# RWKV-7 units of a hybrid flow-matching step cut into jobs that are joined by events, with a matmul order made beside a model of the other engines' queues

## The chip, the core and the metric

The kernel runs on one NeuronCore of a Trainium2 chip. The metric is the device time of one execution in microseconds (us). Engines are named as in the profile: PE (TensorE), DVE (VectorE), ACT (ScalarE), POOL (GpSimd), SP (the queue that issues the DMAs). Each takes its own instructions in order.

## The reference, cut to what matters

One layer is computed for 128 context tokens and 512 latent tokens, 640 columns in all, with width 2048. The combined input projection feeds attention (8 heads) and a bidirectional RWKV-7 mixer (16 heads of 64); both are joined by an output projection, a norm and a SwiGLU feed-forward part.

```python
def _latent_layer(x, c, ckv_ctx, krope_ctx, s_fwd, s_bwd, p):
    sh1, sc1, g1, sh2, sc2, g2 = _adaln(c, p["w_mod"], p["b_mod"])
    proj = (x * (1 + sc1) + sh1) @ p["w_in"]
    ...
    att = _attend_blocked(q_nope, q_rope, ...)
    rw, _, _ = _rwkv_mixer(proj[..., OFF_RW:], s_fwd, s_bwd, p)
    x = _post_norm(x, g1, _merge(att, rw, p), p["ln1_g"], p["ln1_b"])
    x = _post_norm(x, g2, _swiglu(x * (1 + sc2) + sh2, p), p["ln2_g"], p["ln2_b"])
    return x

def step(S, inp):                      # the RWKV scan, one token
    r_t, w_t, k_t, v_t, kk_t, a_t = inp
    sa = jnp.einsum("bhvk,bhk->bhv", S, -kk_t)
    S = S * w_t[:, :, None, :] + sa[..., None] * (kk_t * a_t)[:, :, None, :] + v_t[..., None] * k_t[:, :, None, :]
    return S, jnp.einsum("bhvk,bhk->bhv", S, r_t)
```

The scan is done for both directions; `r_t`, `w_t` and the rest are functions of the projection (token shift, decay and rate through small low-rank products, a normalised key).

## The kernel before, in words

Stages. (1) 0 to about 250 us: the adaLN products `x<-wm,cs`, fed from HBM in pieces, and the first input projection tiles. (2) To about 1145 us: `main()` makes the rest of the input projection, tile by tile (96 matmuls of 128x320 into one `acc` pair of PSUM banks, in three passes of split operands, names `xh`, `xl`, `whi`, `wlo`). Later adaLN products and the RWKV mixer stand between these matmuls. (3) To about 1480 us: attention, and what is left of RWKV. (4) To the end: output projection, norms and the feed-forward part (tiles `b`), with the same code in both kernels.

RWKV. The 16 heads are 8 pairs of 128 rows; each pair is scanned in two halves `j` of 320 columns, so there are 16 units. A unit is scanned in chunks of 64 tokens, five per direction. Its steps: `rwkv_load` (per pair: low-rank weights `lw`, key norm `kk`), `rwkv_decays` (matmuls `m<-xw,lw` and `m<-xa,lw`, then tanh, scan, exp), `rwkv_prep` (DVE and POOL make `nk` and `pr`), `rwkv_grams` (matmuls `m<-pr,nk`, evacuated to `mab`, `mrb`, `pr`), `inverse` (a long row of DVE instructions on `it` and `ip`, ending in `tc`, then matmuls `m<-tc,mab`, `m<-pm,uc`, `m<-t,mab`, `m<-u,pm`), `rwkv_turned` (transposes `sv`, `zv`, `bk`), `rwkv_chain` (five steps in series, each matmuls `m<-sv,pr`, `m<-xs,uf`, `m<-zv,bk` with an evacuation behind each), and per pair `rwkv_bonus` and `rwkv_post` (group norm and gate, `m<-sg,gw`, tile `y`).

What sets the order. PE runs in the order in which the Python program emits its matmuls. That order is made by `Jobs`: every piece of work is a generator with a rank; the one of lowest rank that is ready runs until it yields, and a yielded number is the time after which it may go on. `Tensor` adds a time for each matmul to `now`. In the kernel before, the yielded numbers are constants in `HOPS` (`"prep": 1.68`, `"inv": 12.0`, ...): one number for all that DVE, ACT and POOL do in that step, whatever else stands in their queues. The order of the other engines' instructions is set by a scheduler behind this program, and it too goes by the program's order. A unit starts its prep when the unit ahead has ended its chain: beside a unit run only the decays of the next one, the bonus and the post. Attention has rank 3 and `main` rank 4, so RWKV goes first wherever it is taken to be ready. PSUM: two `acc` pairs, three single banks `m`, one bank `x`.

## Time and profile before

| | |
|---|---|
| time, 3 runs | 3460.67, 3463.75, 3466.30 us; median 3463.75 |
| span of the profiled execution, first to last instruction | 3458.1 us |
| busy share: PE, PE weight load, DVE, ACT, POOL | 94%, 86%, 72%, 42%, 29% |
| mean granted PE clock | 0.969 |
| PE idle 0 to 250 us, 250 to 1375, 1375 to 1480, 1480 to the end | 28.6, 118.4, 10.6, 46.4 us |
| 16 units: first and last prep (tile `nk`) | 254.8 and 1265.0 us |

No other time than its span is given for the profiled execution; it lies 5.65 us under the median of the runs. In the profile a row of a group reads: line, engine, operation, output<-inputs, shape, count | busy us, mean ns of one | idle us of the engine just before them, and what ended it. A float32 matmul of the program stands as two records in the trace. A row of the timeline reads: start us, length us, engine, line, operation, names, shape, count, and in brackets the idle time before it. The rows themselves stand with the prediction.

### The profile page before, as it was taken

The numbers are of one execution on the slowest core, as the hardware profiler recorded it, in microseconds if no ns is written. First come the engines' busy times: TensorE is split into PE (matmuls) and PEld (weight loads), VectorE is DVE, ScalarE is ACT, GpSimd is POOL, SyncE is SP. The second block draws the span as 40 slices with busy tenths as digits, with TensorE's granted clock in tenths as the row PEclk, the third lists the DMA queues.
The fourth block names the chain that finished last, engine by engine and source line by source line (L and its number), as shares of the span: only waits on it lengthen the run. The fifth ranks groups of instructions, "written<-read, shape, count | busy, mean of one in ns | idle before, by whom it ended". The sixth has DMA issues, their size and how long they took to land.

```text
span 3458.1 us, 70966 instructions
## 1 busy us (share of the span) xinstructions
PE 3254.0 (94%) x27682; PEld 2972.3 (86%) x27682; DVE 2499.6 (72%) x4478; ACT 1449.3 (42%) x3031; POOL 999.1 (29%) x1034
## 2 busy tenths in 40 slices
PE   7988988999999789999979999999999999999998
PEld 4677766777887678989979999999999999999997
DVE  1356766776776666467688988888887778899677
ACT  1144443443444444445453444444444444333234
POOL 0022222222222122102174544444443332222124
PEclk9999999999999799999989999999999999999998
DMA  8754444444221211076534443444343357888643
GB/s 300 246 177 136 147 145 139 158 157 144 78 62 56 73 31 40 29 252 185 154 110 138 165 130 122 145 134 129 125 142 116 118 186 282 298 285 288 222 140 120
DMA packets 284528, 527.71 MB, mean 153 GB/s; under 512 B 30432, under 2 KB 66720, under 8 KB 284192
## 3 DMA queue, kind: packets, MB, share of 16 engines
q1 hardware_dynamic: 284192, 523.18, 46.1%
q8 instruction: 217, 3.56, 0.4%
q14 instruction: 119, 0.97, 0.1%
HBM read 428.99 MB, written 92.44 MB: 151 GB/s over the span
## 4 chain that ended last, share of the span: by engine, by line
PE 58%; DVE 6%; ACT 2%; issue 2%; DMA 1%; POOL 1%; SPq 0%; ACTq 0%; DVEq 0%; POOLq 0%
PE b L114 50%; PE acc L114 4%; PE m L114 2%; DVE z L228 1%; DVE ql L228 1%; POOL z L228 1%; PE x L114 1%; ACT z L240 0%; PE acc L118 0%; DVE smx L1165 0%; DVE pr L228 0%; ACT P L1166 0%; DVE ip L228 0%; DVE raw L228 0%; DMA raw<-in_w_down_dram 0%
## 5 line engine op out<-in xcount | busy, mean ns | idle before, releaser
L228 DVE TENSOR_TENSOR ql<-raw,qh 128x512 fp32r<-128x512 f32 (+1 forms) x1064 | 887.8, 849 | 260.4 <-ACT qh L1303 247.1
L1303 ACT CAST qh<-raw 128x512 fp32r<-128x512 f32 (+1 forms) x1064 | 633.3, 610 | 830.6 <-PE b L114 647.2
L114 PE MATMUL b<-t,qh 128*128 128x320 f32 x2816 | 622.8, 310 | 8.5 <-ACT qh L1303 7.4
L228 POOL TENSOR_TENSOR raw<-raw,raw 128x512 f32<-128x512 f32 x240 | 354.4, 1477 | 804.4 <-DVE ql L228 546.2
L114 PE MATMUL b<-op,qh 128*128 128x320 f32 x2560 | 553.2, 311 | 1.9 <-ACT qh L1303 1.1
L114 PEld LDWEIGHTS b<-t,qh 128*128 128x128 f32 x2816 | 472.6, 189 | 9.7 <-ACT qh L1303 8.1
L114 PE MATMUL b<-p,qh 128*128 128x320 f32 x2112 | 468.9, 311 | 0.0
L114 PE MATMUL b<-t,ql 128*128 128x320 f32 x1408 | 436.1, 310 | 5.6 <-DVE ql L228 5.5
L114 PEld LDWEIGHTS b<-op,qh 128*128 128x128 f32 x2560 | 425.9, 189 | 4.4 <-ACT qh L1303 2.7
L114 PE MATMUL b<-op,ql 128*128 128x320 f32 x1280 | 379.0, 311 | 5.4 <-DVE ql L228 5.3
L114 PEld LDWEIGHTS b<-p,qh 128*128 128x128 f32 x2112 | 356.0, 189 | 0.3
L114 PE MATMUL b<-p,ql 128*128 128x320 f32 x1056 | 329.0, 312 | 6.9 <-DVE ql L228 6.9
L114 PEld LDWEIGHTS b<-t,ql 128*128 128x128 f32 x1408 | 265.0, 188 | 7.8 <-DVE ql L228 7.7
L114 PEld LDWEIGHTS b<-op,ql 128*128 128x128 f32 x1280 | 236.7, 189 | 8.3 <-DVE ql L228 7.9
L114 PE MATMUL b<-mh,qh 128*128 128x320 f32 x1024 | 230.4, 314 | 6.6 <-ACT qh L1303 6.6
L114 PE MATMUL acc<-xh,whi 128*128 128x320 f32 x928 | 230.3, 330 | 3.5 <-ACT P L1166 2.5
L114 PE MATMUL acc<-xl,whi 128*128 128x320 f32 x928 | 232.9, 333 | 0.0
L114 PE MATMUL acc<-xh,wlo 128*128 128x320 f32 x928 | 231.8, 332 | 0.0
L114 PEld LDWEIGHTS b<-p,ql 128*128 128x128 f32 x1056 | 199.8, 189 | 9.6 <-DVE ql L228 9.6
L228 DVE TENSOR_TENSOR raw<-raw,raw 128x512 f32<-128x512 f32 x240 | 185.4, 780 | 12.5 <-POOL raw L228 9.4
L265 ACT CAST whi<-raw 128x512 fp32r<-128x512 f32 (+1 forms) x156 | 94.9, 609 | 226.4 <-PE acc L114 138.9
L114 PEld LDWEIGHTS b<-mh,qh 128*128 128x128 f32 x1024 | 174.5, 191 | 8.3 <-ACT qh L1303 7.8
(330 smaller groups left out, 5654.5 us busy)
## 6 DMA issues: line engine op xcount, KB each, us to landing
wm<-in_w_mod_dram SPq DMA_DIRECT2D x64, 1024.0 KB, 5.3
raw<-in_w_gate_dram SPq DMA_DIRECT2D x188, 256.0 KB, 2.7
raw<-in_w_up_dram SPq DMA_DIRECT2D x188, 256.0 KB, 2.9
op<-hd SPq DMA_DIRECT2D x136, 320.0 KB, 5.4
raw<-in_w_in_dram SPq DMA_DIRECT2D x132, 256.0 KB, 2.7
wm<-in_w_mod_dram SPq DMA_DIRECT2D x64, 512.0 KB, 6.0
raw<-in_w_out_dram SPq DMA_DIRECT2D x128, 256.0 KB, 3.0
raw<-in_w_down_dram SPq DMA_DIRECT2D x128, 256.0 KB, 5.4
```

The lines of the kernel that those rows point to most:

```text
L114: self.eng.matmul(out, lhsT, rhs, start=start, stop=stop)
L228: eng.tensor_tensor(out=out, in0=x, in1=y, op=op)
L265: A.copy(hi, r)
L1303: A.copy(hi, x)
```

## The change

Jobs. `rwkv()` is replaced by `rwkv_chains` (rank 0), `rwkv_inverses` (0.3), `rwkv_turn` (0.5), `rwkv_fed` (prep and grams, 0.6), `rwkv_inputs` and `rwkv_rest` (1). Each goes through the 16 units by itself and waits for events of the others, so the chain of one unit, the inverse of the next and prep or decays of the one after may stand between each other. The grams go to an `acc` pair while `main` runs, not to two of the three `m` banks. The states are loaded in `rwkv_turned`, not in the chain; `r` and `v` of a pair are loaded later than `k`. More buffers: `N_S` 14 for 12, `N_W` 8 for 6; the DMA scratch is smaller.

Times in the planner. `V`, `A` and `G` are wrapped in `Lane`, which keeps the time at which that engine's queue will be empty, from an overhead and a rate per element; a job yields `left(...)`, the time until the queues it has fed are empty. `inverse` and `rwkv_decays` yield after each DVE step. `Tensor` has other times per matmul and adds 0.093 us where the shape of the array's tile changes.

Every engine has the same instructions as before by count and kind, apart from the banks of 13 of 16 units' grams.

```diff
-N_S = 12
+N_S = 14
-N_W = 6
+N_W = 8
+RANK_F = 0.3
+RANK_G = 0.6
...
+class Lane:
+    def __init__(self, eng, pe, fixed, rate):
+        self.eng, self.pe, self.fixed, self.rate, self.free = eng, pe, fixed, rate, 0.0
+    def __getattr__(self, name):
+        f = getattr(self.eng, name)
+        def call(*args, **kw):
+            n = 0
+            for x in (kw.get("out", args[0] if args else None), kw.get("in_")):
+                if x is not None:
+                    n = max(n, math.prod(x.shape[1:]))
+            self.free = max(self.free, self.pe.since) + self.fixed + self.rate * n
+            return f(*args, **kw)
+        return call
...
-    V, A, G, DMA = nc.vector, nc.scalar, nc.gpsimd, nc.sync
+    V, A, G = Lane(nc.vector, T, 0.1, 1.2e-3), Lane(nc.scalar, T, 0.1, 1.05e-3), Lane(nc.gpsimd, T, 0.15, 2.5e-3)
+    def left(*lanes, more=0.15):
+        return max(x.free for x in lanes) - T.now + more
...
     def inverse(...):
-        yield HOP["inv"]
+        yield left(V)
...
-        yield HOP["prep"]
+        yield left(V, A, G)
...
-        yield HOP["pow"]
+        yield left(V, G, more=1.5)
...
     def rwkv_grams(u):
-            both = [mps(), mps()]
+            if mg.done:
+                both = [mps(), mps()]
+            else:
+                pair = acc()
+                both = [pair[:, h, :] for h in range(2)]
...
-    def rwkv():
...
+    def rwkv_fed():
+        for u in UNITS:
+            yield decayed[u]
+            if before(u):
+                yield turns[before(u)]
+            yield from rwkv_prep(*u, shs[u[0]], us[u])
+            prepped[u].done = True
+            yield from rwkv_grams(us[u])
+            grammed[u].done = True
+            jobs.spawn(rwkv_turn(u), TURN)
+    def rwkv_turn(u):
+        if before(u):
+            yield chained[before(u)]
+        yield from rwkv_turned(*u, shs[u[0]], us[u])
+        turns[u].done = True
+    def rwkv_inverses():
+        for u in UNITS:
+            yield grammed[u]
+            us[u]["u"] = yield from inverse(us[u]["mab"], chained[before(u)] if before(u) else None)
+            inverted[u].done = True
+    def rwkv_chains():
+        for u in UNITS:
+            yield turns[u]
+            yield inverted[u]
+            yield from rwkv_chain(*u, shs[u[0]], us[u])
+            chained[u].done = True
```

What moves, at three places. First, PE ahead of the first unit's grams (`pr`, `nk`); before:

```order
L114 MATMUL acc_155<-xl_1365,whi_1992 128x320 x2
L114 MATMUL acc_155<-xh_1364,wlo_1993 128x320 x2
L114 MATMUL acc_155<-xh_1373,whi_1992 128x320 x2
L114 MATMUL acc_155<-xl_1374,whi_1992 128x320 x2
L114 MATMUL m_2111<-pr_2077,nk_2076 128x128
L114 MATMUL m_2112<-pr_2078,nk_2076 128x128
```

and now:

```order
L118 MATMUL acc_2110<-xl_1026,whi_2155 128x320 x2
L118 MATMUL x_2174<-wm_403_2175,cs 32x512 x4
L118 MATMUL acc_2110<-xh_1366,whi_2206 128x320 x2
L118 MATMUL acc_2260<-pr_2180,nk_2179 128x128
L118 MATMUL acc_2260<-pr_2181,nk_2179 128x128
```

Between the last decay matmul (`xl`, `lw`) and these grams stood 11 such `acc` rows and one `x<-wm` row; now there are 49 `acc` rows, three `x<-wm` rows and one `x<-cst,ev` row, and the grams write `acc`, not `m`.

Second, PE in the chain of the first unit (`xs`, `zv`, `sv` are its tiles, `uf` its inverse; `tc`, `pm`, `t` are those of the next unit's inverse, `vr` its transposes); before, from one step's second product to its third and on:

```order
L114 MATMUL m_2856<-xs_2839,uf_166 64x64 x4
L114 MATMUL acc_2566<-xh_1025,whi_2654 128x320 x2
L114 MATMUL acc_2566<-xl_1026,whi_2654 128x320 x2
L114 MATMUL acc_2566<-xh_1025,wlo_2655 128x320 x2
L114 MATMUL m_2869<-zv_2290,bk_2291 64x64 x4
L114 MATMUL acc_2566<-xh_1346,whi_2762 128x320 x2
```

and now:

```order
L118 MATMUL m_3377<-xs_3344,uf_166 64x64 x4
L118 MATMUL m_3385<-tc_3361,mab_2790 32x32 x40
L118 MATMUL m_3427<-zv_2382,bk_2383 64x64 x4
L118 MATMUL m_3436<-pr_2180,sv_2381 64x64
L118 MATMUL m_3436<-pr_2181,sv_2381 64x64
L118 MATMUL m_3437<-pr_2180,sv_2381 64x64
L118 MATMUL m_3437<-pr_2181,sv_2381 64x64
L118 MATMUL m_3436<-mrb_2259,zv_2382 64x64 x2
L118 MATMUL m_3437<-mrb_2259,zv_2382 64x64 x2
L118 MATMUL m_3449<-pm_3384,uc_3325 32x32 x40
L118 MATMUL m_3502<-cst,v_2153 64x64 x10
L118 MATMUL x_3117<-wm_588_3333,cs 32x512 x4
```

A chain step, whose places in between were taken by projection matmuls, now shares them with the next unit's inverse.

Third, DVE in a chain (`zv`, `sv`, `fs`, `y` of the chain; `ip`, `it`, `ue` of an inverse; `ld` of decays); before, in the second unit:

```order
L237 SCALAR_TENSOR_TENSOR sv_3137<-m_3578,dc_2382,sd_3558 64x64 x4
L228 TENSOR_TENSOR wlo_3592<-raw_3506,whi_3591 128x512
L228 TENSOR_TENSOR y_2669<-m_3609,y_2669 128x64
L228 TENSOR_TENSOR y_2669<-m_3610,y_2669 128x64
L896 COPY zv_3138<-m_3621 64x2x64
L237 SCALAR_TENSOR_TENSOR sv_3137<-m_3634,dc_2382,sd_3606 64x64 x4
```

and now, in the fifth:

```order
L148 SCALAR_TENSOR_TENSOR fs_6357<-m_6523,dc_4959,sd_6466 64x64
L148 TENSOR_REDUCE it_6411<-ip_6575 128x2x7
L148 TENSOR_TENSOR ip_6593<-im_6481,it_6411 128x512
L148 TENSOR_REDUCE it_6411<-ip_6593 128x8x8
L148 TENSOR_TENSOR ip_6651<-it_6411 128x512
L148 TENSOR_SCALAR ld_6535<-ld_6535 128x640
L148 TENSOR_REDUCE it_6411<-ip_6651 128x8x8
L148 COPY zv_5763<-m_6586 64x2x64
```

Between one step's state update and the next step's `zv` there was at most a `wlo` and two small `y`; now rows of the sixth unit's inverse and the decays of a third stand there.

More of the change, by code (lines that the diff above doesn't have):

```diff
@@ L100, in __init__, with matmul @@
     def __init__(self, eng):
-        self.eng, self.now = eng, 0.0
-    def matmul(self, out, lhsT, rhs, start, stop, share=1.0):
+        self.eng, self.now, self.last, self.since = eng, 0.0, None, 0.0
+    def matmul(self, out, lhsT, rhs, start, stop):
         n = 1
@@ L145, in step @@
         job = min((j for j in free if j.ready <= now), key=lambda j: j.rank)
-        self.pe.now = now
+        self.pe.now, self.pe.since = now, job.ready
         try:
@@ L556, in step_kernel, with inverse @@
         G.memset(t, 0.0)
-    def inverse(mab):
+    def inverse(mab, before):
         par = [con("par")[:, i: i + 1] for i in range(2)]
@@ L571, in inverse @@
         G.memset(tb[:, 0:256:17], 1.0)
+        yield left(V, A)
         x = half5("ix")
         V.transpose(x, nd)
+        yield left(V, more=0.0)
         x3 = x.rearrange("p (t s) -> p t s", s=32)
@@ L578, in inverse @@
         stt(m3, x3[:, :, 0:16], par[0], m3, ALU.mult, ALU.add)
+        yield left(V, more=0.0)
         t3 = tb[:, :256].rearrange("p (t s) -> p t s", s=16)
@@ L586, in inverse @@
             V.tensor_reduce(out=t8[:, :, t, 0:t], in_=pd, op=ALU.add, axis=AX.X)
+            yield left(V, more=0.0)
         lo8, hi8 = slice(0, 8), slice(8, 16)
@@ L621, in inverse @@
         u, t = h10(u2[:, :HN]), h10(t2[:, :HN])
-        yield HOP["d32b"]
+        yield left(V)
+        if before:
+            yield before
         f4 = ch(full)
@@ L639, in inverse @@
         for lo, hi in lohi:
+            A.copy(f4[lo, :, 0:32], u[lo])
+        for lo, hi in lohi:
             A.copy(f4[lo, :, 32:64], h10(ps2[lo, :HN]))
-        yield HOP["d64b"]
+        yield left(A)
         return full
@@ L706, in rwkv_load, with rwkv_load2 @@
         sh["ks"] = slot("ks")
-        yield HOP["kk"]
+        yield left(V)
         return sh
+    def rwkv_load2(i, sh):
+        for j, n in ((0, "r"), (2, "v")):
+            sh[n] = slot(n)
+            DMA.dma_start(out=sh[n], in_=rkv_d[i][j])
     HV = [slice(0, HN), slice(HN, NT)]
@@ L777, in rwkv_turned @@
         sv_, zv, bk = u["sv"], u["zv"], u["bk"] = wide("sv"), wide("zv"), wide("bk")
-        yield HOP["vr"]
+        for h in range(2):
+            if j == 0:
+                for d, e in ((0, 0), (1, 7)):
+                    DMA.dma_start(out=sv_[rows(h), e, h, :], in_=a["states"][d, i, rows(h)])
+                G.memset(sv_[rows(h), 5, h, :], 0.0)
+            else:
+                G.tensor_copy(sv_[rows(h), 0:6:5, h, :], cy[rows(h)].rearrange("p (d v) -> p d v", v=C))
+                G.memset(sv_[rows(h), 3, h, :], 0.0)
+        yield left(A)
         for d in range(2):
@@ L839, in rwkv_chain @@
             sh["y"] = slot("y")
-        for h in range(2):
-            if j == 0:
-                for d, e in ((0, 0), (1, 7)):
-                    DMA.dma_start(out=sv_[rows(h), e, h, :], in_=a["states"][d, i, rows(h)])
-                G.memset(sv_[rows(h), 5, h, :], 0.0)
-            else:
-                G.tensor_copy(lanes(sv_, h, 0), lane2(cy, h))
-                G.memset(sv_[rows(h), 3, h, :], 0.0)
         y = sh["y"]
@@ L908, in rwkv_chain @@
             if e < 4:
-                yield HOP["p"]
+                yield left(V)
         outputs(4)
@@ L950, in rwkv_post @@
             tt(V, y[:, hs], y[:, hs], ps[:, :HN], ALU.mult)
-            yield HOP["gup"]
+            yield left(V)
         DMA.dma_start(out=mix_d[8 + i], in_=y)
-    def rwkv():
-        def start(i):
+    UNITS = [(i, j) for i in range(npairs) for j in range(2)]
+    shs = [None] * npairs
+    us = {}
+    decayed, prepped, turns, grammed, inverted, chained = ({u: jobs.event() for u in UNITS} for _ in range(6))
+    posted, summed_ = ([jobs.event() for _ in range(npairs)] for _ in range(2))
@@ L972, in rwkv @@
-        sh, u = yield from start(0)
-        last = None
-        for i in range(npairs):
-            for j in range(2):
-                yield from rwkv_prep(i, j, sh, u)
-                yield from rwkv_grams(u)
-                turned = jobs.spawn(rwkv_turned(i, j, sh, u), TURN)
-                side = jobs.spawn(beside_second(i, sh) if j else beside_first(i, sh, last), RANK_S)
-                u["u"] = yield from inverse(u["mab"])
-                yield turned
-                yield from rwkv_chain(i, j, sh, u)
-                last = (i, sh)
-                yield side
-                if side.result:
-                    sh, u = side.result
```

143 lines of the change are left out of this document (94 added, 49 removed).

## The prediction

> **What bounds the kernel now.** I read the head of the page first, then a table by stages, then the groups of PE with the idle time before them, and last single waits.
>
> ```profile
> PE 3254.0 (94%) x27682; PEld 2972.3 (86%) x27682; DVE 2499.6 (72%) x4478; ACT 1449.3 (42%) x3031; POOL 999.1 (29%) x1034
> ...
> PEclk9999999999999799999989999999999999999998
> ...
> PE 58%; DVE 6%; ACT 2%; issue 2%; DMA 1%; POOL 1%; SPq 0%; ACTq 0%; DVEq 0%; POOLq 0%
> ```
>
> PE is busy for 94% of the span of 3458.1 us and makes most of the chain that ended last, so time can come from two places only: PE's idle 204 us, and what a low granted clock adds to its busy time. By stages (columns: stretch, its length, busy us of each engine, granted clock, DMA share, GB/s):
>
> ```profile
> 0.00:250.00 250.00, 221.40 (x1266) 149.16 (x1267) 87.44 (x172) 61.31 (x117) 14.50 (x45) 0.96 0.72 243
> 250.00:1035.00 785.00, 713.86 (x9171) 572.72 (x9169) 542.43 (x1197) 341.26 (x884) 187.70 (x316) 0.96 0.40 130
> 1035.00:1145.00 110.00, 99.59 (x1224) 84.87 (x1222) 70.58 (x161) 49.63 (x127) 29.65 (x42) 0.93 0.24 76
> 1145.00:1375.00 230.00, 193.15 (x2384) 164.96 (x2384) 157.77 (x360) 104.26 (x261) 53.62 (x79) 0.91 0.12 37
> 1375.00:1480.00 105.00, 94.42 (x693) 89.17 (x691) 44.35 (x93) 43.62 (x99) 18.15 (x24) 0.98 0.13 40
> 1480.00:3458.00 1978.00, 1931.62 (x12952) 1911.43 (x12952) 1596.99 (x2499) 849.27 (x1544) 695.47 (x528) 0.98 0.53 174
> ```
>
> The last row, 57% of the span, is the feed-forward part, where the change leaves code and order alone. The RWKV units fill 250 to 1375 us (rows two to four): PE is idle there for 71.1 + 10.4 + 36.9 = 118.4 us, and with (1 − clock) x busy time the clock costs about 0.04 x 714 + 0.07 x 100 + 0.09 x 193 = 53 us. So 171 us is all that the change can reach, and no engine is full there: DVE has 542 + 71 + 158 = 771 us of 1125. Which waits make the idle time (groups of PE from 250 to 1375 us; behind the bar busy us, mean ns | idle us before them and what ended it):
>
> ```profile
> L114 PE MATMUL m<-pr,nk 64*128 64x128 f32 x640 | 59.7, 295 | 29.2 <-DVE nk L228 9.0 <-DVE y L228 9.0 <-POOL sv L847 8.3
> ...
> L114 PE MATMUL m<-zv,bk 128*64 128x64 f32 x576 | 37.7, 240 | 5.2 <-DVE zv L896 5.2
> ...
> L114 PE MATMUL m<-xs,uf 64*64 64x64 f32 x640 | 34.7, 227 | 4.8 <-ACT xs L874 4.8
> ...
> L114 PE MATMUL x<-cst,ev 128*128 128x2 f32 x120 | 16.8, 262 | 7.0 <-DVE ev L356 6.0 <-DVE it L586 1.1
> ...
> L114 PE MATMUL m<-tc,mab 32*32 32x32 f32 x1280 | 15.8, 204 | 17.1 <-DVE tc L601 17.0
> ...
> L114 PE MATMUL m<-t,mab 32*32 32x32 f32 x640 | 14.1, 197 | 6.6 <-DVE t L228 6.3 <-issue 0.3
> ...
> L114 PE MATMUL m<-sg,gw 128*128 128x320 f32 x28 | 11.4, 492 | 3.8 <-DVE y L228 3.8
> ...
> L114 PE MATMUL m<-xa,lw 128*128 128x320 f32 x30 | 11.4, 380 | 9.5 <-DVE y L228 9.5
> ...
> L114 PE MATMUL m<-qr,rot 128*128 128x512 f32 x6 | 3.7, 699 | 4.9 <-ACT qr L240 4.9
> ```
>
> Grams, the inverse's first product and the products behind `y` hold half of it; the chain's own hand-offs (`zv,bk` and `xs,uf`) hold only 10 us. What one wait does to the clock (timeline of PE: start, length, instruction, idle time before; then one stretch of the stage table):
>
> ```profile
> 252.19 0.46 PE L114 MATMUL acc<-xh,whi 128*128 128x320 f32 x2
> 252.49 0.46 PE L114 MATMUL acc<-xl,whi 128*128 128x320 f32 x2
> 261.94 2.90 PE L114 MATMUL m<-pr,nk 64*128 64x128 f32 x16 [8.99 <-DVE nk L228]
> ...
> 265.46 0.73 PE L114 MATMUL acc<-xh,whi 128*128 128x320 f32 x2
> 266.00 0.73 PE L114 MATMUL acc<-xl,whi 128*128 128x320 f32 x2
> ```
>
> ```profile
> 262.00:268.00 6.00, 5.91 (x28) 5.35 (x28) 2.62 (x4) 2.93 (x8) 1.29 (x1) 0.50 0.01 4
> ```
>
> Two projection matmuls take 0.30 us ahead of the wait of 8.99 us (252.19 to 252.49) and 0.54 behind it, with the clock at 0.50. So a long wait is paid twice, and a projection matmul placed ahead of it is worth 0.15 us of cover.
>
> **The change, part by part.** The instructions are the same; what differs is what stands between a producer and its consumer. The planner's numbers for prep and inverse rise from 1.68 and 12.0 to times kept per queue, and the places are filled with projection matmuls.
>
> *Grams.* In the first unit 11 rows of two projection matmuls and one adaLN row cover prep: 22 x 0.15 + 1 (1.06 in a row below) = 4.3 us, and PE then waited 9.0, so prep needs 13.3. Now 49 such rows and three adaLN rows stand there: 98 x 0.15 + 3 = 17.7 us. The wait goes with 4 us to spare. The 9.0 behind `y` and the 8.3 marked `sv` are waits for an `m` bank; grams of 13 units now take an `acc` pair. I leave 3 of 29.2: **−26** (bounds −29 and, if `acc` is held as long, −9).
>
> *Inverse.* Its DVE row, timeline of DVE in the third unit, first, two of the longest and last instruction:
>
> ```profile
> 406.84 0.45 DVE L567 COPY nd<-mab 32x320 f32<-32x320 f32 x1
> ...
> 417.30 1.05 DVE L228 TENSOR_TENSOR ip<-im,it 128x512 f32<-128x512 f32 x1
> ...
> 425.05 0.48 DVE L601 STREAM_TRANSPOSE tc<-uc 128x320 f32<-128x320 f32 x1
> ```
>
> From 406.84 to 425.53 it is 18.7 us, where the constant said 12. By the rows between the last gram and `tc,mab`, PE had 17 to 18 us of work ahead and now has some 32. Waits of 17.0 become 2: **−15** (bounds −17 and 0, since DVE now shares that time with a chain).
>
> *Products behind `y`.* The hold of `m` by `y` is as it was, but decays no longer stand straight behind it; grams have left these banks. Of 9.5 + 3.8 I take half: **−6** (0 to −13).
>
> *Chains.* This is where the change puts what it takes away. A chain step goes PE, ACT, DVE (`zv`), PE, DVE (`sv`), as in these rows of the second unit; below them, in the fifth unit's inverse, what it looks like when another job is in DVE's queue:
>
> ```profile
> 381.36 0.99 DVE L237 SCALAR_TENSOR_TENSOR sv<-m,dc,sd 64x64 f32<-64x64 f32 x4 [0.94 <-PE m L114]
> ...
> 383.94 0.29 DVE L896 COPY zv<-m 64x128 f32<-64x128 f32 x1 [0.30 <-ACT zv L895]
> ```
>
> ```profile
> 566.94 0.49 DVE L234 TENSOR_SCALAR ld<-ld 128x640 f32<-128x640 f32 x1 [1.89 <-ACT ld L240]
> 567.47 1.54 DVE L731 TENSOR_TENSOR_SCAN ld<-cst,ld 128x320 f32<-128x320 f32 x2
> 568.92 0.87 DVE L237 SCALAR_TENSOR_TENSOR nb<-ta,kk 128x320 f32<-128x320 f32 x2
> 569.71 0.48 DVE L228 TENSOR_TENSOR t<-m,tc 128x320 f32<-128x320 f32 x1
> ```
>
> In that second fence `t`, which PE needs, comes out behind 2.9 us of decays, and ahead of them DVE itself waits 1.89 us for ACT. Counting DVE's instructions between a chain's first and last `zv` in both orders, with durations from the rows of before, gives 140 us over 16 units before and 302 now: 162 us of inverse, prep and decays stand there in addition. PE's work over the same places, first to fifth `xs,uf`, grows from 245 to 373 us. So on the sum DVE has room; unit by unit its work exceeds PE's in six of 16, by about 16 us together. I take **+16**. Bounds: 0, if the places are so chosen that each DVE instruction falls into a gap; +81, if PE waits for half of the 162.
>
> *Power on POOL.* PE's product behind `rt` has 2.1 to 2.4 us of other work ahead, where it had 4.5 to 5.1:
>
> ```profile
> L228 POOL TENSOR_TENSOR rt<-st,mhalf 128x10 f32<-128x10 f32 x15 | 30.6, 2037 | 205.9 <-DVE st L232 110.9 <-DVE st L234 65.4 <-DVE it L586 15.1
> ```
>
> 2.04 us and its DVE step of about 0.3 need 2.4: some 0.3 us in 16 cases, **+5** (0 to +10).
>
> *Shapes.* A row of another array shape starts later behind its neighbour:
>
> ```profile
> 430.41 0.46 PE L114 MATMUL acc<-xh,wlo 128*128 128x320 f32 x2
> 430.70 0.45 PE L114 MATMUL acc<-xh,whi 128*128 128x320 f32 x2
> 431.09 1.06 PE L114 MATMUL x<-wm,cs 128*32 128x512 f32 x8
> ```
>
> 0.39 us instead of 0.29. The order changes shape 1029 times ahead of the feed-forward part, before 956: 73 x 0.1 = **+7**.
>
> *Clock.* The groups with long waits (the groups above but `zv,bk` and `xs,uf`) hold 78 us; of these 47 go. I let the clock's loss shrink by nearly the same share, 53 to 23: **−30** (0 to −43). The Trainium skill ("TensorE: Matmul & The Clock Gate", Part 1, The HAM clock gate) says that PE falls to half rate after an idle window of about 3.4 us and comes back after a busy one; the 0.50 behind 8.99 us agrees. By that rule what I leave, nearly all of it under 2 us, would not throttle, and the sum would be some 20 us lower.
>
> *At nothing:* earlier loads of states, later ones of `r` and `v`, the smaller DMA scratch, the start-up and attention, where PE keeps nearly the order it had (0 ± 5). The loads land while the unit ahead runs its chain; uncovered, a load of this kind costs about what this row of the DMA issues has last (us to landing), in eight pairs some 20 us:
>
> ```profile
> raw<-in_w_in_dram SPq DMA_DIRECT2D x132, 256.0 KB, 2.7
> ```
>
> Sum: −26 −15 −6 +16 +5 +7 −30 = −49. 3458.1 − 49 = 3409. The median of the runs is 5.65 us above the profiled span; carried over, that gives **3415 us**.
>
> **The rivals.**
>
> *A, the sum above.* With the terms' bounds taken together half way, 3380 to 3440.
>
> *B, nearly all waits go.* The cover is now worked out per queue; if that is right on the whole, idle time falls from 118 to 40 (attention's waits, `ev` and what banks hold stay) and the clock's loss to 10: −78 −43 +7 = −114, so 3350 us. For it: DVE has 354 us free of 1125 in this stretch. Against: the time kept for DVE goes by the program's order, while DVE's own order is set behind it, and one such misplacement costs 2.9 us above.
>
> *C, the waits only move.* A unit has about 164 projection matmuls as filler in both orders. If the work that covered chains now covers inverses, each gain above returns in the chains: +47 and +30 there. Within 0.2% (6.9 us, about what a measurement of this kernel can tell), 3463 us. Against: filler that covers two jobs at a time counts twice.
>
> *D, DVE becomes the limit in the chains; slower.* Each chain has five steps in series, and each passes DVE twice in order. If PE waits for half of the 162 us, the chain term is +81 in place of +16; waits of 1 to 3 us would then be many, and I give back only half of the clock: −47 +81 +5 +7 −15 = +31, so 3495 us. It decides from a chain term of 50 us on. For it: six of 16 units have more DVE than PE work, and rows like that of 566.94. Against: `inverse` and decays now yield after each DVE step, so short pieces of 0.3 to 1.7 us are what a `zv` can find ahead of it. The Trainium skill ("SBUF — State Buffer", Who interferes with whom) says that a DVE instruction with two SBUF inputs contends with a GpSimd instruction that reads SBUF, one blocking for the other's whole length; prep would meet chains on these engines more often. No run shown here separates that.
>
> **How the numbers follow.** A 0.53, B 0.22, C 0.10, D 0.15. The likeliest gives 3415 us. The range takes in B (3350) with some room, A and C, and stops where D would need more than half its price: 3340 to 3478. Faster: A and B, 0.75, and a little of C: 0.76; same 0.09; slower 0.15.
>
> **What would show it.** Grams without a wait for `nk`, and under 5 us in all; the group `m<-tc,mab` at about 2 us; `m<-xa,lw` and `m<-sg,gw` near 7 together. If D is right, `m<-zv,bk` and `m<-sv,pr` carry tens of us with DVE as releaser; in A about 20 to 25. The product behind `rt` should carry some 5 us released by POOL. The granted clock of the RWKV stretch should rise from 0.91 to 0.96 to about 0.98. The feed-forward part should keep its 1978 us; if it moves by over 5 us, the sum was made on the wrong stretch. The forecast is wrong if the waits of inverses go and the end comes no sooner, or if the waits in chains come to over 50 us.

## The result, and the profile after

The changed kernel takes 3500.62 us (median of 3 runs, 3500.21 to 3503.9), the kernel before 3463.75 us. The ratio is 1.0107, with a 95% interval of 1.0089 to 1.0125: slower by about 37 us. The forecast was 3415 us, faster, with a range up to 3478. The profiled execution after has a span of 3502.1 us, 44.0 us more than that of before. It lies 1.5 us above the median of its runs, that of before 5.65 us under its median, so the sums below, made from these two spans, come to more than 37.

Three lines of the page after: engines, granted clock in 40 slices, and the chain that ended last.

```profile
PE 3281.7 (94%) x27682; PEld 2994.2 (85%) x27682; DVE 2486.9 (71%) x4478; ACT 1446.9 (41%) x3031; POOL 997.0 (28%) x1034
...
PEclk9999989999999899999999999999999999999998
...
PE 70%; DVE 12%; ACT 4%; issue 3%; DMA 3%; POOL 1%; SPq 0%; ACTq 0%; DVEq 0%; POOLq 0%
```

PE is busy as large a share as before, but for 27.7 us longer, with the same 27682 instructions. DVE's share of the last chain has doubled (6% to 12%) and DMA's has tripled. By stages, with the border at the first feed-forward matmul (1481 us before, 1521 after); before:

```profile
250.00:1481.00 1231.00, 1101.16 (x13468) 911.87 (x13466) 815.24 (x1809) 539.58 (x1372) 289.11 (x461) 0.95 0.31 100
1481.00:3458.00 1977.00, 1931.48 (x12952) 1911.29 (x12952) 1596.88 (x2499) 848.46 (x1543) 695.47 (x528) 0.98 0.53 174
```

and after:

```profile
250.00:1521.00 1271.00, 1126.07 (x13441) 932.57 (x13439) 802.48 (x1804) 534.89 (x1369) 288.93 (x458) 0.93 0.30 97
1521.00:3502.00 1981.00, 1931.24 (x12952) 1910.50 (x12952) 1593.84 (x2499) 849.07 (x1544) 691.88 (x528) 0.98 0.53 173
```

The feed-forward part is within 4 us of what it was. The 40 us lie in the stretch with RWKV and attention: PE busy 25 us longer at a lower clock (0.95 to 0.93), and 15 us more of idle time. Which waits (groups of PE in that stretch, after):

```profile
L118 PE MATMUL acc<-pr,nk 64*128 64x128 f32 x520 | 43.0, 304 | 33.5 <-ACT mrb L148 33.0 <-ACT ain L148 0.5
L118 PE MATMUL m<-zv,bk 128*64 128x64 f32 x576 | 41.1, 243 | 16.0 <-DVE zv L148 13.6 <-ACT zv L148 2.4
L118 PE MATMUL m<-pr,sv 128*64 128x64 f32 x640 | 38.1, 232 | 13.0 <-ACT mrb L148 4.2 <-DVE kk L148 4.0 <-ACT ld L148 2.5
L118 PE MATMUL m<-xs,uf 64*64 64x64 f32 x640 | 37.1, 236 | 4.1 <-ACT xs L148 2.7 <-DVE y L148 1.4
...
L118 PE MATMUL m<-cst,rt 128*64 128x128 f32 x300 | 21.9, 297 | 3.7 <-POOL rt L148 3.6
L118 PE MATMUL x<-cst,ev 128*128 128x2 f32 x120 | 20.4, 292 | 19.4 <-DVE ev L148 19.4
L118 PE MATMUL m<-pm,uc 32*32 32x32 f32 x1280 | 15.6, 194 | 8.4 <-issue 5.9 <-DVE pm L148 2.2 <-ACT y L148 0.2
L118 PE MATMUL m<-tc,mab 32*32 32x32 f32 x1280 | 14.6, 196 | 0.4 <-ACT y L148 0.4
...
L118 PE MATMUL m<-sg,gw 128*128 128x320 f32 x32 | 11.5, 441 | 0.0
L118 PE MATMUL m<-xa,lw 128*128 128x320 f32 x30 | 10.1, 338 | 1.6 <-ACT mrb L148 1.1 <-DVE zv L148 0.2
```

The inverse's first product waits 0.4 us where it waited 17.1, and the products behind `y` 1.6 where they waited 13.3. In their place stand grams in front of `acc` (33.5, all behind ACT's evacuation `mrb`), `x<-cst,ev` (19.4 for 7.0), and the chain products `zv,bk`, `pr,sv`, `xs,uf` (33.1 for 10.0; `pr,sv` waited for nothing before).

**How idle time and clock add up.** The records give the stretches in which the clock was 0.50. Half of PE's busy time in them is what the clock cost. From the start to the first feed-forward matmul:

| | idle | clock's loss | rest | sum |
|---|---|---|---|---|
| before | 158.4 | 59.7 | 1262.7 | 1480.9 |
| after | 170.9 | 84.8 | 1265.7 | 1521.4 |
| difference | +12.5 | +25.1 | +3.0 | +40.6 |

The rest, PE's work at the full clock, hardly moves: in all the runs below it lies between 1256 and 1274 us. So two thirds of the loss is clock. Half-clock stretches between 250 us and the feed-forward part went from 19 to 31, although the longest waits are shorter (the two longest are 6.5 and 6.4 us, before 9.0 and 8.6). One such stretch (timeline of PE, after):

```profile
473.52 1.16 PE L118 MATMUL acc<-pr,nk 64*128 64x128 f32 x16 [1.49 <-ACT mrb L148]
...
477.15 1.06 PE L118 MATMUL x<-wm,cs 128*32 128x512 f32 x7 [1.18 <-issue]
478.15 0.56 PE L118 MATMUL acc<-xl,whi 128*128 128x320 f32 x2
481.05 1.23 PE L118 MATMUL acc<-pr,nk 64*128 64x128 f32 x8 [2.35 <-ACT mrb L148]
...
486.65 0.73 PE L118 MATMUL acc<-xl,whi 128*128 128x320 f32 x2
487.18 0.74 PE L118 MATMUL acc<-xh,wlo 128*128 128x320 f32 x2
```

No wait here is longer than 2.35 us, yet from 479.4 us on the clock is 0.50, and projection pairs start 0.53 apart (486.65 to 487.18). What ACT did at that time:

```profile
477.04 0.83 ACT L148 ACTIVATE kk<-k,vec 128x640 f32<-128x640 f32 x1 [2.60 <-DMA k<-rkv]
477.89 0.36 ACT L148 COPY mab<-acc 64x256 f32<-64x256 f32 x1
...
479.14 0.37 ACT L148 COPY mrb<-acc 64x256 f32<-64x256 f32 x1
```

ACT stood for 2.60 us in front of the load of `k` with the evacuation of the grams behind it; PE's wait names `mrb`, but in this stretch it begins with a DMA, for which the planner had allowed 3.0 us. And on DVE, some 15 us later:

```profile
496.71 1.04 DVE L148 STREAM_TRANSPOSE uc<-ue 128x512 f32<-128x512 f32 x1
497.78 0.51 DVE L148 STREAM_TRANSPOSE tc<-uc 128x320 f32<-128x320 f32 x1
498.33 0.29 DVE L148 COPY zv<-m 64x128 f32<-64x128 f32 x1
```

```profile
498.68 0.69 PE L118 MATMUL m<-zv,bk 128*64 128x64 f32 x6 [4.24 <-DVE zv L148]
```

A chain's `zv` stands behind the end of the next unit's inverse, and PE waits 4.24 us, the longest wait of a chain.

### The profile page after: what moved, and what is told of

Read it like the earlier page. It is cut to its first block, busy times and chain, and to the rows that moved or that the text cites. A ratio compares the mean times of both kernels' runs of the same rounds, so it can differ in the third digit from the quotient of the medians.

```text
span 3502.1 us, 70905 instructions
## 1 busy us (share of the span) xinstructions
PE 3281.7 (94%) x27682; PEld 2994.2 (85%) x27682; DVE 2486.9 (71%) x4478; ACT 1446.9 (41%) x3031; POOL 997.0 (28%) x1034
## 4 chain that ended last, share of the span: by engine, by line
PE 70%; DVE 12%; ACT 4%; issue 3%; DMA 3%; POOL 1%; SPq 0%; ACTq 0%; DVEq 0%; POOLq 0%
PE b L118 49%; PE acc L118 11%; PE m L118 7%; PE x L118 2%; DVE z L148 1%; DVE ip L148 1%; DVE ql L148 1%; DVE pr L148 1%; DMA raw<-in_w_down_dram 1%; DVE it L148 1%; POOL z L148 1%; DVE wlo L148 1%; DMA k<-rkv 1%; DVE nk L148 1%; DMA wm<-in_w_mod_dram 0%
## 5 line engine op out<-in xcount | busy, mean ns | idle before, releaser
L148 DVE TENSOR_TENSOR wlo<-raw,whi 128x512 fp32r<-128x512 f32 (+1 forms) x156 | 112.9, 724 | 133.0 <-ACT whi L148 113.2
```

The source lines that it names most:

```text
L148: return f(*args, **kw)
```

## The experiments

In each table line: the median; the ratio to the kernel before on the same chip with its 95% interval; and, from the trace, idle time and clock's loss up to the feed-forward part, as in the table above (before 158.4 and 59.7, after 170.9 and 84.8).

| run | us | ratio | idle | loss |
|---|---|---|---|---|
| e1 grams on `m` | 3517.69 | 1.0141 (1.0123 to 1.0160) | 160.5 | 116.3 |
| e2 longer load times | 3489.34 | 1.0060 (1.0043 to 1.0077) | 155.0 | 86.4 |
| e3 before, two constants | 3470.07 | 1.0007 (0.9996 to 1.0018) | 156.1 | 73.0 |
| e4 inverse held back | 3525.27 | 1.0160 (1.0143 to 1.0178) | 169.2 | 109.1 |
| e6 model, no overlap | 3632.18 | 1.0468 (1.0445 to 1.0491) | 250.7 | 147.8 |
| e7 paced, after | 3503.67 | 1.0103 (1.0084 to 1.0122) | 167.8 | 77.2 |
| e8 paced, before | 3468.46 | 1.0003 (0.9990 to 1.0015) | 157.5 | 60.2 |
| e9 overlap, no model | 3593.40 | 1.0375 (1.0359 to 1.0390) | 223.0 | 130.1 |
| e10 early loads and `ev` | 3477.17 | 1.0033 (1.0019 to 1.0048) | 159.2 | 69.8 |
| e11 before, grams on `acc` | 3500.58 | 1.0108 (1.0093 to 1.0123) | 190.7 | 66.4 |
| e12 second group on `m` | 3495.59 | 1.0094 (1.0069 to 1.0119) | 149.3 | 91.1 |
| e13 early loads alone | 3501.55 | 1.0103 (1.0083 to 1.0123) | 164.3 | 91.4 |
| e14 e10 and e12 | 3483.26 | 1.0048 (1.0031 to 1.0064) | 148.1 | 88.1 |
| e15 e14, power and `kk` later | 3440.52 | 0.9934 (0.9911 to 0.9956) | 137.2 | 70.1 |
| e16 power alone | 3483.54 | 1.0058 (1.0043 to 1.0073) | 156.5 | 79.8 |
| e17 e15, grams on `acc` | 3483.57 | 1.0063 (1.0046 to 1.0080) | 158.6 | 73.1 |
| e18 e15, `kk` at 9 | 3487.22 | 1.0065 (1.0050 to 1.0080) | 150.2 | 91.9 |

### The gram banks: e1, e11, e12

e1, in the changed kernel:

```diff
-            if mg.done:
+            if True:
                 both = [mps(), mps()]
```

> The changed kernel with the grams of all units in two of the three m banks, as before, PE's order unchanged. Theory banks: while the projection holds one acc pair, the three gram groups of a unit follow each other through the only other pair and each waits until the one ahead is evacuated; this made the 33.5 us of idle in front of acc<-pr,nk. Then the group m<-pr,nk falls to about 15 us, the time by 20 to 35 us (3465 to 3480, with the clock's share). Theory queue: the evacuation itself is late, because ACT, which does it, stands in front of a load; then the waits stay near 30 us under another name, perhaps more behind y, and the time is 3490 to 3510.

The groups of PE in e1:

```profile
L118 PE MATMUL m<-pr,nk 64*128 64x128 f32 x640 | 65.3, 338 | 6.2 <-DVE fs L148 3.5 <-ACT pm L148 2.0 <-DVE y L148 0.2
...
L118 PE MATMUL m<-xw,lw 128*128 128x320 f32 x30 | 12.8, 426 | 7.5 <-ACT mrb L148 7.4
L118 PE MATMUL m<-xa,lw 128*128 128x320 f32 x30 | 12.3, 411 | 10.9 <-ACT mrb L148 8.1 <-DVE zv L148 1.2 <-DVE sv L148 1.1
```

The grams' waits fall from 33.5 to 6.2 us, as theory banks said; 16 us of them come back as decays that wait for an `m` bank (the two rows behind, 2.9 us in the changed kernel). Idle time is 10 us less than in the changed kernel, and the time is still longer, by 17 us of the medians and 12 of the ratios, because the clock's loss grows by 31.5. Neither theory named that. Between these two kernels the clock outweighs idle time by three to one.

e11 makes the same swap the other way round, alone, in the kernel before:

```diff
-            both = [mps(), mps()]
+            if mg.done:
+                both = [mps(), mps()]
+            else:
+                pair = acc()
+                both = [pair[:, h, :] for h in range(2)]
```

> The kernel before with the grams in an acc pair while the projection runs, nothing else. Theory banks: the waits of grams behind y and sv (17 of 29 us) go, but groups now wait for each other; idle time falls by 5 to 15 us, 3445 to 3462. Rival: no gain, as the second and third group wait for the one free pair: within 5 us of the kernel before.

Two groups of PE in e11, and then the first of them in the kernel before:

```profile
L114 PE MATMUL acc<-xh,whi 128*128 128x320 f32 x864 | 219.9, 337 | 15.1 <-ACT u L411 8.2 <-ACT P L1170 2.5 <-ACT ain L512 2.5
...
L114 PE MATMUL acc<-pr,nk 64*128 64x128 f32 x552 | 52.9, 310 | 54.5 <-ACT mrb L820 34.6 <-DVE nk L228 9.0 <-POOL sv L851 8.3
```

```profile
L114 PE MATMUL acc<-xh,whi 128*128 128x320 f32 x871 | 216.4, 330 | 3.5 <-ACT P L1166 2.5 <-DVE vS L1158 1.0
```

Both theories were wrong: it is 37 us slower, mostly by idle time (158.4 to 190.7). Each gram group waits for the one ahead in the one free pair (34.6 of 54.5 behind `mrb`), and the next projection tile has to wait for its pair (15.1 for 3.5). So `acc` is the better place by 12 us (difference of the ratios) in the changed kernel, and the worse by 37 us in the kernel before: a bank has no price of its own; it depends on what stands beside it.

e12, the changed kernel with only the second of three groups on `m`:

```diff
-            if mg.done:
+            if mg.done or e0 == 4:
```

> The changed kernel in which only the second of a unit's three gram groups goes back to two m banks, so that two groups in a row never need the same acc pair. Theory banks (the three groups queue for one pair): the idle time of the gram groups falls from 33 to about 20 us, the time to 3485 to 3492. Theory m (three m banks are full with two chains' worth of work, so each gram group there makes others wait, as when all went there): no gain, 3497 to 3512.

The grams' waits go almost wholly (33.5 to 1.5 us), further than theory banks said, but the time ends between the two theories: idle time falls by 21.6 us, the clock's loss rises by 6.3, and the median is 5 us below that of the changed kernel, which lies within the interval. So the gram banks do cause the gram waits, but these waits alone do not make the kernel slower.

### The loads ahead of ACT: e2, e13, e10

e2:

```diff
-        yield 2.0
+        yield 5.0
         A.copy(lw, raw)
...
-        yield 3.0
+        yield 9.0
         act(kk, k, AF.Square, scale=vcol("kk", i))
```

> The changed kernel with longer times in the planner for two loads of a pair (2.0 to 5.0 us ahead of the copy lw<-raw, 3.0 to 9.0 us ahead of kk<-k), nothing else. Theory queue: ACT waits 27 us for these DMAs with evacuations of grams and inverses behind it. Then ACT's waits for DMA fall below 5 us, the idle time in front of acc<-pr,nk and x<-cst,ev falls by 10 to 20 us and the time by 15 to 30 us (3470 to 3485). Theory banks: the waits of grams stay above 28 us, and the time stays within 6 us of 3500.

The waits of grams (33.5 to 20.1) and of `x<-cst,ev` (19.4 to 15.2) fell as theory queue said, the time by less: 11 us, where it gave 15 to 30. Its cause is there only in part: ACT's wait for `k` went (6.7 to 0), that for the low-rank weights stayed (19.9 and 19.4). In the trace their load is mostly issued when DVE's `wlo<-raw,whi` has freed a `raw` buffer, so a longer time in the planner does not bring it forward. e13 takes nearly all of both away, with a buffer of its own for these weights (and `N_S` 13 for 14, to make room):

```diff
-N_S = 14
+N_S = 13
...
-        raw = load_raw(a["lora"][i])
+        raw = lraw.pop() if lraw else lora_in(i)
...
-        yield 2.0
         A.copy(lw, raw)
...
-        yield 3.0
+        yield 9.0
...
+        if i + 1 < npairs:
+            lraw.append(lora_in(i + 1))
```

> The changed kernel with the two loads made early (own buffer for the low-rank weights, 9 us ahead of kk<-k) and N_S 13, but with the old 1.0 us ahead of x<-cst,ev. If ACT's wait for the loads is what the version with all three gained by, 3475 to 3485 with x<-cst,ev still at 10 us or more; if the ev time was the larger half, 3488 to 3498.

3501.55 us, outside what either case gave: ACT's waits for these two loads fall from 26.6 to 4.6 us and nothing is gained (idle time 6.6 us less, clock's loss 6.6 more). So ACT standing in front of a DMA, which a single stretch of the timeline shows so plainly, is not by itself what made the kernel slower, though e2, which takes only `k`'s wait away, gained 11 us. e10 is e13 with one more line in the planner, for the copy ahead of the small adaLN products:

```diff
-        yield HOP["ev"]
+        yield left(V)
```

> The changed kernel with the low-rank weights of the next pair loaded a pair ahead into a buffer of their own, 9 us in the planner ahead of kk<-k, and the modelled DVE queue in place of 1.0 us ahead of x<-cst,ev (N_S is 13 for 14, to make room for the buffer). Theory queue: ACT's waits for these DMAs fall from 27 us below 4, grams and ev wait 15 to 25 us less, the time is 3470 to 3485. Rival: what was behind these loads on ACT waits for DVE anyway; idle time falls by less than 8 us and the time stays above 3490.

Groups of PE, first e13, then e10:

```profile
L118 PE MATMUL acc<-pr,nk 64*128 64x128 f32 x536 | 48.2, 324 | 29.4 <-ACT mrb L148 26.0 <-ACT u L148 3.1 <-issue 0.3
...
L118 PE MATMUL x<-cst,ev 128*128 128x2 f32 x120 | 19.0, 279 | 18.6 <-DVE ev L148 18.5
```

```profile
L118 PE MATMUL acc<-pr,nk 64*128 64x128 f32 x520 | 47.3, 326 | 25.7 <-ACT mrb L148 25.2 <-issue 0.3
...
L118 PE MATMUL x<-cst,ev 128*128 128x2 f32 x120 | 16.3, 257 | 7.5 <-DVE ev L148 7.4
```

With the load waits gone, this line is worth 24 us: `x<-cst,ev` waits 11 us less, of which 5.1 are left in the sum of all idle time, and the clock's loss falls by 21.6. The prediction had taken the group `x<-cst,ev` as untouched; its constant of 1.0 us was nearly enough before (7.0 us of waits) and far too short where an inverse may stand in DVE's queue.

### Overlap and model, each alone: e4, e6, e9

e4 holds the inverse back until the chain ahead is done:

```diff
             yield grammed[u]
+            if before(u):
+                yield chained[before(u)]
```

> The changed kernel with the inverse of a unit held back until the chain of the unit ahead is done; prep, grams, decays, loads still run beside a chain. Theory chain: the inverse's DVE row in the chains is what makes PE wait in front of m<-zv,bk, m<-pr,sv, m<-xs,uf and m<-sv,pr (35 us, against 11 in the kernel before). Then these fall by 15 us or more and the clock's loss with them: 3465 to 3485. Rival: the waits in chains come from decays, prep and the DMA waits just as much; they fall by less than 8 us, and the time stays within 10 us of 3500 or rises, since a unit's steps are again in series.

```profile
L118 PE MATMUL m<-zv,bk 128*64 128x64 f32 x576 | 44.2, 248 | 18.8 <-DVE zv L148 15.0 <-ACT zv L148 3.3 <-DVE y L148 0.2
L118 PE MATMUL m<-pr,sv 128*64 128x64 f32 x640 | 40.3, 236 | 10.5 <-ACT xs L148 5.4 <-ACT ld L148 3.0 <-DVE kk L148 1.3
...
L118 PE MATMUL m<-cst,rt 128*64 128x128 f32 x300 | 26.4, 338 | 20.7 <-POOL rt L148 20.7
```

The rival held. With no inverse beside a chain, `zv,bk` waits 18.8 us, not less than 16.0, and the four chain products together 35.3 us, where they waited 34.6. The wait of 4.24 us above is an inverse's; the sum of such waits is not.

e6 lets a unit's prep wait for the chain ahead (`yield chained[before(u)]` in place of `turns` in `rwkv_fed`), with the model kept; e9 keeps the events and takes the constants and the matmul times of the kernel before, without the yields between DVE steps.

> The changed kernel in which a unit's prep waits for the chain of the unit ahead, so that beside a chain only decays, loads, bonus and post of others run, as in the kernel before; the planner's model of the queues, its times and the banks stay as changed. Theory overlap (three units side by side are what costs): 3450 to 3475. Theory model (the order made beside the modelled queues packs small work and leaves the filler to long waits): 3490 or more.

> The changed kernel's jobs, events and gram banks with the planner of before: the constants of the kernel before in place of the modelled queues (prep 1.68, inverse 12 us and so on), its times per matmul, no yields between the DVE steps. This is the overlap without the model. Theory longer times (the model's longer times stretch each unit and three units side by side only earn that back): a unit takes less than the 66 us of before, the chains end before 1400 us, and the time is 3440 to 3475. Rival (the overlap itself fills the queues of ACT and DVE, and the model was what kept it in bounds): idle time above 160 us, 3510 or more.

Both are far slower than either kernel, 1.0468 and 1.0375. In e6 the chains of 16 units need 1301 us from the first `xs,uf` (333.0) to the last (1634.0), where before they needed 1051 and after 1105: the modelled times stretch a unit, and overlap is what earns most of it back. The chain products wait 24.2 us in e6, 11.0 of them for DVE, against 20.6 in the changed kernel and 19.4 in e4: DVE's share of these waits falls when prep is held back too, and not when the inverse alone is. In e9 the grams alone wait 75.4 us, 32 of them for prep itself (`nk`, `pr`), which 1.68 us in the planner does not cover:

```profile
L116 PE MATMUL acc<-pr,nk 64*128 64x128 f32 x640 | 76.5, 375 | 75.4 <-ACT mrb L138 31.8 <-DVE nk L138 20.5 <-POOL pr L138 11.3
```

So neither half of the change pays by itself. Theory overlap, that e6 would land at the kernel before, was wrong and theory model held; theory longer times was wrong for e9, and its rival held (idle time over 160 us, 3510 or more).

### Filler: e3, e7, e8

e3 gives the kernel before two constants of the changed table:

```diff
-"prep": 1.68, ... "inv": 12.0
+"prep": 6.5, ... "inv": 17.0
```

> The kernel before with two of its constants raised to the values in the changed table: prep 1.68 to 6.5 and inverse 12 to 17 us. No overlap of units. Theory covers: the long waits for nk and tc (26 us) are a matter of these two numbers alone; the two groups fall by 15 to 25 us, the clock's loss by 10 to 20, and the time is 3425 to 3445. Rival (the waits move): a unit's filler is the same, so the chains wait instead, and the time is within 10 us of 3463.

No difference (1.0007): the rival held. The wait for `tc` falls from 17.1 to 6.9 us and that of the grams from 29.2 to 18.2, and the chains (11.0 to 22.5), `acc<-kh,qh` in attention (7.4 to 16.8), `m<-t,mab` (6.6 to 11.9) and the clock's loss (59.7 to 73.0) take it all back: the products of `xh` end at 1366 us in place of 1450 and the last chain at 1467 in place of 1363, so more of RWKV stands without filler. This is rival C of the prediction, that the waits only move, in the kernel before.

e7 and e8 add a rule that makes projection matmuls follow each piece of RWKV work, 0.8 us per us in the changed kernel with e2's times, 0.5 in the kernel before:

```diff
         job = min((j for j in free if j.ready <= now), key=lambda j: j.rank)
+        if self.debt > 0:
+            job = next((j for j in free if j.ready <= now and j.rank == RANK_M), job)
```

> The changed kernel with the longer load times of the run before, and a rule in the planner: each us of RWKV work on PE is followed by 0.8 us of projection matmuls, as long as there are any ready, before the next RWKV work. Theory clock (bare stretches of small matmuls and short waits make the clock fall): the clock's loss falls from 80 to 50 us, idle time stays, 3455 to 3475. Rival: filler spent at once is missing in the long waits and at the end; idle time grows by 20 us or more and the time is 3490 to 3520.

> The kernel before with the same rule at 0.5 us per us, nothing else. Theory clock: the clock's loss falls from 52 to 40 us at the same idle time, 3445 to 3460. Rival: long waits for nk and tc get less cover, idle time grows by more than the clock gives, 3470 to 3490.

Against e2 the rule lowers the clock's loss by 9 us and raises idle time by 13: the rival by its time, with less idle time than it gave. In the kernel before neither sum moves, though the waits do: those in the chains grow from 11.0 to 40.5 us and others fall by as much.

### What the clock answers to: e5

e5 appends matmuls behind the last PE work of the kernel before. It was executed once. Its span is 4110.3 us, some 650 us more and not the 350 that were meant.

> The kernel before with some 350 us of matmuls appended behind its last PE work, the same code ahead of them. Stretches of some 24 us of dense 128x320 matmuls separate: about 35 us of 32x32 matmuls in the inverse's pattern and 30 us of 64x64 ones without a wait; then groups of 24, 12, 8, 5 and 3 dense matmuls with one hand-off to ACT and back (1 us or less of idle) between; then the same with 80 and 40 of the 32x32 and four of the 64x64. Theory mix (small matmuls count in part as idle, by a fit over the windows of the traces so far 0.2 to 0.45 of their time): the two stretches of small matmuls without waits keep the full clock or nearly, dense groups of 24 and 12 keep it, those of 3 lose it (idle 60%), and the small groups with a hand-off are at 0.5 to 0.7. Theory idle (only idle time counts, from about half of a 3.4 us window on): dense and small groups lose the clock at the same share of idle time.

Stretches of it (length, PE busy, and so on; granted clock third from the end):

```profile
3484.00:3560.00 76.00, 39.05 (x2599) 36.31 (x2588) 0.00 (x0) 0.00 (x0) 0.00 (x0) 0.50 0.02 4
3587.00:3607.00 20.00, 20.00 (x692) 20.00 (x690) 0.00 (x0) 0.00 (x0) 0.00 (x0) 1.00 0.02 4
...
3792.00:3815.00 23.00, 16.95 (x87) 12.46 (x86) 0.00 (x0) 3.60 (x17) 0.00 (x0) 1.00 0.00 1
3841.00:3851.00 10.00, 6.80 (x30) 4.26 (x30) 0.00 (x0) 1.91 (x9) 0.00 (x0) 1.00 0.01 2
3852.00:3869.00 17.00, 13.08 (x36) 8.65 (x34) 0.00 (x0) 2.33 (x11) 0.00 (x0) 0.50 0.00 0
4067.00:4083.00 16.00, 10.51 (x124) 7.61 (x120) 0.00 (x0) 3.18 (x15) 0.00 (x0) 0.50 0.00 1
```

Three rows of its timeline, groups of five and of three dense matmuls with one hand-off between, the last one after the clock has fallen:

```profile
3811.53 0.99 PE L114 MATMUL b<-pq 128*128 128x320 f32 x5 [0.36 <-ACT sc L1957]
...
3850.38 0.71 PE L114 MATMUL b<-pq 128*128 128x320 f32 x3 [0.36 <-ACT sc L1957]
3851.44 1.17 PE L114 MATMUL b<-pq 128*128 128x320 f32 x3 [0.36 <-ACT sc L1957]
```

Groups of five are idle 0.36 of each 1.35 us, 27%, and keep the clock for 23 us. Groups of three are idle 0.36 of 1.06 us, 34%, and lose it after some 10 us (from 3851 us on 0.50). Half-clock stretches last whole multiples of 3.41 us in every trace here (774 of 793; the others are the last of a trace, which its end cuts off), so I cut the trace into such windows. Those in the groups of five hold up to 1.07 us of idle time, and all are followed by the full clock. The first two in the groups of three hold 1.07 us too and are forgiven; the third holds 1.16 and is not. No single wait was over 0.38 us. So the sharpest border seen is about a third of a window, not the half that theory idle had put there. Groups of the 64-column product (row 4067, 0.37 idle after 0.45) lose the clock; the same product without a wait keeps it (row 3587). The 32x32 stretches (row 3484) lose it too, but PE runs dry there, so theory mix, that small matmuls count as part idle, is neither shown nor excluded by them.

The same holds in the kernels, with a less sharp border. I cut 250 us to the feed-forward part into the clock's windows of 3.41 us and counted how many of those at the full clock were followed by one at half clock, by the idle time in them:

| idle time in the window | before | after | all 20 traces |
|---|---|---|---|
| under 1 us | 1 of 278 | 1 of 267 | 54 of 5435 |
| 1.0 to 1.5 us | 5 of 30 | 7 of 25 | 115 of 460 |
| 1.5 us or more | 13 of 15 | 23 of 27 | 391 of 459 |

A full-clock window followed by a half-clock one is called a fall of the clock here. That is the step from 19 to 31 stretches: 27 windows in place of 15 with 1.5 us or more of idle time in them. In 21 of these 27 it is a single wait. Seven falls of the clock in each kernel lie beside a wait of 3.41 us or more; the other 12 before and 24 after have only shorter ones. Waits of 1.5 to 3.4 us rose from 15 (28.2 us together) to 24 (51.2 us), while those above fell from 41.5 to 28.3 us.

The one exception before, the window from 947.3 us on, has no idle time at all by the records, but ten records of a product with two columns (1.28 us) and ten with one column (1.25 us). This is what theory mix would give; one window does not show it.

### A version below both: e14 to e18

e14 joins e10 and e12. e15 is e14 with two numbers in the planner changed:

```diff
-        yield left(V, G, more=1.5)
+        yield left(V, G, more=2.5)
...
-        yield 9.0
+        yield 12.0
         act(kk, k, AF.Square, scale=vcol("kk", i))
```

> Early loads, modelled ev and the second gram group in m banks together. Theory banks: 3455 to 3468, level with the kernel before. Theory m: 3478 or more, no better than without the banks.

> The version before, with 1 us more in the planner for POOL's power (1.5 to 2.5 us above its queue) and 12 in place of 9 us ahead of kk<-k. m<-cst,rt falls from 7 to below 2 us, m<-krs,rot from 9 to 5; 3 to 10 us below the version before it, which would be below the kernel before.

e14 is no better than e10: theory m held. e15 takes 3440.52 us, 0.9934 (0.9911 to 0.9956) of the kernel before and 60 us below the changed one. The stage row shows it (to the feed-forward part, now at 1471):

```profile
250.00:1471.00 1221.00, 1107.19 (x13408) 917.23 (x13407) 805.74 (x1801) 531.55 (x1365) 284.40 (x454) 0.94 0.31 100
```

Idle time is 21 us below the kernel before; the clock's loss is still 10 above. The gain over e14 was expected at 3 to 10 us and is 43. What made it:

> The changed kernel with one number changed in the planner, 2.5 in place of 1.5 us above the queue of POOL's power (two places). If that was the effective part of the version that came out below the kernel before: 3450 to 3475. If it only worked with the early loads: 3490 to 3505. By the price of the prediction (5 us): 3495.

> The version that came out below the kernel before, but with all gram groups in acc pairs as changed. Theory banks: 12 to 20 us longer than it (3452 to 3462), the groups acc<-pr,nk waiting some 25 us again. Otherwise within 6 us of it.

> The same version with 9 in place of 12 us ahead of kk<-k: what the power's time alone gives on top of early loads and split banks. If the power is it: 3440 to 3450; if the later kk was it: 3475 to 3485.

e16 changes the power's number alone in the changed kernel: 3483.54, 17 us better, between the cases named, and mostly not at its own product (`m<-cst,rt` waits 4.8 us, before the edit 3.7). e18 is e15 with 9 for 12 us ahead of `kk`: 3487.22, so neither is the power's number the reason by itself. e17 is e15 with the grams on `acc`: 3483.57. Each of the three steps back from e15 (e14, e17, e18) loses 43 to 47 us. For e17 the trace names a wait; groups of PE, first e17, then e15:

```profile
L118 PE MATMUL acc<-pr,nk 64*128 64x128 f32 x536 | 46.1, 314 | 31.3 <-ACT mrb L148 31.3
```

```profile
L118 PE MATMUL m<-pr,nk 64*128 64x128 f32 x312 | 27.4, 305 | 1.2 <-DVE fs L148 0.6 <-ACT mrb L148 0.4 <-ACT ld L148 0.2
```

All grams wait 31.7 us in e17 and 1.2 in e15, and idle time is 21.4 us more: theory banks by its wait, though the time rose by 43 us and not by 12 to 20. So e12's edit, which gave 5 us to the changed kernel and nothing to e10, is worth 43 here. For e14 and e18 no wait that I can name is worth the step: no group moved by more than 7 us, and the clock's loss is 18 and 22 us more. The order as a whole changes with each number, and these runs scatter over 20 to 45 us with it. Which property of e15's order is the good one stays open.

## Why the prediction was wrong, point by point

The likeliest case was a gain of 49 us. It failed by its sign. Rival D gave the right sign and nearly the right time (3495), but by luck: it needed a chain term of 50 us or more, and the chains' waits grew by 24; and it still let the clock's loss shrink by 15 us, where it grew by 25.

- **Grams, −26 forecast, +4 measured (29.2 to 33.5 us).** The wait for `nk` went, as worked out. The step that failed is the one that counted an `acc` pair as free: three groups in a row need the one pair that the projection leaves, and wait behind `mrb`. The bound of −9 "if `acc` is held as long" was too kind. e11 shows this alone: +25 us of gram waits.
- **Inverse, −15 forecast, −17 measured.** Right. e3 shows that a constant alone does much of it, and that it pays nothing where the filler ends earlier.
- **Products behind `y`, −6 forecast, −12 measured.** Right, larger.
- **Chains, +16 forecast, +24 measured** (`zv,bk`, `pr,sv`, `xs,uf`, `sv,pr`: 11.0 to 34.6). The size was fair. The reason given, inverse, prep and decays together in DVE's queue, holds in part: some 20 of the 34.6 us are waits for DVE. The inverse alone is not it, for e4 took it away and the waits stayed; prep and decays were not separated. D's +81 did not happen.
- **Power, +5 forecast, +3.7 measured** at its own product. But e16 shows that this number moves the time by 17 us through the order of everything else.
- **At nothing.** `x<-cst,ev` was not looked at, though it stands in the adaLN work that the change moves: +12 us, and e10 against e13 shows 24 us with the clock. `m<-pm,uc` added 6.
- **Shapes, +7 forecast.** No run measures this term alone; all of PE's work at the full clock, in which it is contained, grew by 3.
- **Clock, −30 forecast, +25 measured.** The largest error, 55 of the 93 us between forecast (−49) and result (+44) of the span. The step that failed is "I let the clock's loss shrink by nearly the same share" as the long waits. The probe and the windows show what it missed: the clock falls without a long wait, when a third to a half of a window is idle. The change cut waits of 9 and 8.6 us, each of which costs one fall, and put in their place nine more waits of 1.5 to 3.4 us, most of which cost one fall each too. The trace of before could have told: 12 of its 19 falls have no wait of 3.4 us beside them. The Trainium skill ("TensorE: Matmul & The Clock Gate", A second HAM failure mode: psum-queue depth-cycling) says of another kernel that PE idling briefly and often between groups of matmuls makes the clock swing; 36 of 42 windows with 1.5 us of idle time or more agree. Its rule in Part 1, The HAM clock gate, an idle window of about 3.4 us, which the prediction cited, does not hold here as the prediction read it: groups of three, never idle for over 0.36 us at a time, lost the clock.

Of what the prediction named as signs: the inverse near 2 us and the products behind `y` under 7 came; grams under 5 and a clock of 0.98 did not; the feed-forward part stayed within 4 us.

## What to carry to other kernels

Write time as PE's work plus idle time plus what a low clock adds; here the first never moved by 1%, and the third was the larger part of the change. To keep the clock, look at how much of each 3.41 us PE stands still, not at the longest wait: one wait of 9 us costs one fall of the clock, while six of 1.5 us in six windows would cost about five (an estimate, from the 36 of 42 above). And where an order is planned by numbers, one number is not one term: edits of 1 to 3 us in the planner moved this kernel by 17 to 47 us, and sums over the waits they touch missed that (3 to 10 us expected for e15, 43 measured). A bank or a buffer has to be priced in the kernel where it is used.

## What the hardware showed that was not expected

Dense 128x320 matmuls with 27% idle in gaps of 0.36 us keep the clock at 1.00 (up to 1.07 us of idle time in 3.41 us), and with 34% lose it (1.16 us). And a long row of independent 32x32 products ran dry again and again (timeline of e5):

```profile
3478.78 1.52 PE L114 MATMUL b<-pf 32*32 32x32 f32 x157
3482.58 1.93 PE L114 MATMUL b<-pf 32*32 32x32 f32 x128 [2.28 <-issue]
3486.32 1.93 PE L114 MATMUL b<-pf 32*32 32x32 f32 x128 [1.82 <-issue]
```

After 157 records without a pause PE waits 1.5 to 2.3 us ahead of every further 128, which come with about as many weight loads (2599 and 2588 in the stretch of 76 us above). The profile shows nothing that it waits for and calls it issue. In the RWKV units the same name stands for 5.9 of the 8.4 us of `m<-pm,uc`, a row of 40 products (80 records) of that shape: six waits, all inside the row, behind 34 to 74 of its records. That the two have one cause was not tested.
